# Attention products in a hybrid mLSTM and attention block: float32 against three float16 passes

## The chip, the cores and the metric

One core of a Trainium2 chip runs the whole program. The metric is the time of one execution in device microseconds; the program is one layer of a streaming encoder over 512 tokens of width 2048, with a final norm.

## The reference, cut to what matters

The layer normalises x, modulates it by a conditioning vector, and multiplies by one wide input matrix `w_in`. Its columns feed an mLSTM branch (4 heads of 256), an attention branch (8 heads of 128) and two merge gates. Each branch has an output projection; the merged sum goes through `w_out` and is added to x. Of the attention branch, this is what the change touches:

```python
def chunk_attention_branch(aq, ak, av, az, rel_bias):
    q = to_heads(aq, A_HEADS) * (A_HEAD_DIM ** -0.5)
    ...
        s = jnp.einsum('bhqd,bhkd->bhqk', qj, kb).astype(jnp.float32) + bias
        s = jnp.where(valid, s, -jnp.inf)
        p = jax.nn.softmax(s, axis=-1)
        return jnp.einsum('bhqk,bhkd->bhqd', p.astype(vb.dtype), vb)
    ...
    return from_heads(out) * jax.nn.silu(az)
```

## The kernel before, in words

The large products are already made from two float16 parts of each operand: a value is scaled by a power of two, its high part is rounded to float16, and the low part is what is left. `split` (L142) makes them, ACT the high part at L143 and DVE the low part at L144, which reads the high one. Three passes, high by high, high by low and low by high, are accumulated in one PSUM bank.

A prelude, up to some 165 us, streams `w_ada` and makes the modulation, the normalised h and, in float32, seven first column blocks (`PRE`: q, k and z of heads 0 and 1, and q of head 2). From then on the work runs in units (`plan`, L47). A unit is a block of weights of 1 MB: loaded, squared and summed for its scale (L179, L127, L134 to L139), split, and multiplied with h. `feat_mm` (L394) gives a feature by token result in 48 matmuls of 512 columns, `tok_mm` (L412) a token by feature result in 96 matmuls of 256 columns. The unit "if" (L679) makes the mLSTM's eight gate columns with 192 matmuls of 8 columns. Weights are loaded six units ahead and split four units ahead.

The pipeline (L800 to L822) does for unit i, in program order: its products on PE (`gemm`), the evacuation of unit i − 1 (`evac`), then the side work's steps of the phase "A" (ACT and DVE), the loads, squares and splits for later units, the small matmul for their scales, and last the side work's steps of the phase "P" (PE). So a PE step of the side work stands between two units, and its ACT and DVE step runs beside the next unit's products. The tile framework orders each engine's queue from this program; it may put one unit's splits ahead of side work.

Attention (L442) is such side work. For a head: four score matmuls in float32, for query tiles of 128 rows against the 128, 256, 384 and 512 keys up to them (L463); in the next step the addition of the bias, the maximum, the exponential with its sum, and the scaling (L470 to L476); then ten transposes of probabilities in float32 (L483); then their copies out of PSUM into a part of the array `B` (ACT at L490, DVE at L492, two each, of 512, 384, 256 and 128 columns); then four products with v in float32 (L500); then the product with the gate z (L504). The scores use four of the four banks of one PSUM pool, which transposes and products use after them.

q is evacuated by DVE at L701 with both its scales and the factor of the attention, k by ACT at L704, v by ACT at L714 (two parts for a pair of heads), z at L706 to L709. `times` (L114) makes one-column scale products. At head 6 the attention waits for the gate unit and runs the mLSTM's decays, which are many small float32 matmuls (L526 to L539), before it goes on; the mLSTM's heads follow it. The rest (mLSTM, merge, output projection) isn't touched.

Of the kernel before, what the change touches and what calls it, by code (L numbers as in the profile page):

```python
# [19 lines left out]
P = 128  # L20
# [26 lines left out]
def plan():  # L47
    """The pieces of weights in the order of their use: (kind, index, part)."""
    u = []
    for kind, h in ATT:  # L50
        u += [(kind, h, 0), (kind, h, 1)] if kind == "v" else [(kind, h, 0)]
    for h in range(M_H):
        for kind in ("mq", "mk", "mv", "mo", "mz"):
            u += [(kind, h, 0), (kind, h, 1)]
    for d in range(0, KT, 2):
        u += [("ga", d, 0), ("ga", d + 1, 0), ("pa", d, 0), ("gm", d, 0), ("gm", d + 1, 0), ("pm", d, 0)]
    for b in range(8):
        u += [("out", b, 0), ("out", b, 1)]
    return u


PAIRS = ("v", "mv", "out")
VC = M_DH + 2


@with_exitstack
def block_kernel(ctx: ExitStack, tc: tile.TileContext, A, out):
# [26 lines left out]

    # Two arrays that change their content: one holds the split h, later the split merged branches;
    # the other x and h, then the branches' outputs y, in single tiles of 512 columns.
    hsp = big.tile([P, 2, KT, S], F16, tag="A", name="hsp")
# [16 lines left out]
    def times(a, col, imm, name, n=1):  # L114
        t = small.tile([P, n], F32, tag=f"tm{n}", name=f"tm_{name}", bufs=16)
        if col is None:
            V.tensor_scalar(t, a, imm, None, ALU.mult)
        else:
            V.tensor_scalar(t, a, col, imm, ALU.mult, ALU.mult)
        return t  # L120

# [1 line left out]
    def tot_of(cols, name, tot=None):  # L123
# [6 lines left out]
    def scale_of(tot, name, pool=None):  # L130
        """From a sum of squares: 2^e by which the operand is multiplied, and 2^-e."""
        pool = pool or small
        u = small.tile([P, 1], U32, tag="u", name=f"u_{name}")
        V.tensor_scalar(u, tot[:, 0:1].bitcast(U32), 24, None, ALU.logical_shift_right)  # L134
        kw = {} if pool is const else {"bufs": 12}
        sc = pool.tile([P, 1], F32, name=f"sc_{name}", **({} if pool is const else dict(tag="sc", **kw)))
        V.tensor_scalar(sc.bitcast(I32), u, -8388608.0, 204.0 * 8388608.0, ALU.mult, ALU.add)  # L137
        inv = pool.tile([P, 1], F32, name=f"inv_{name}", **({} if pool is const else dict(tag="inv", **kw)))
        V.tensor_scalar(inv.bitcast(I32), u, 8388608.0, 50.0 * 8388608.0, ALU.mult, ALU.add)  # L139
        return sc, inv  # L140
# [4 lines left out]

# [1 line left out]
    units = plan()  # L147
# [59 lines left out]

# [1 line left out]
    att_pool = tc.tile_pool(name="att", bufs=1)  # L209
# [17 lines left out]
    def ada_load(g, n):  # L227
        """The next n pieces of the columns of w_ada that make shift and scale of a group of tiles."""
        ks = groups[g]
        total = 4 if len(ks) == 2 or ks[0] == KT - 1 else 2  # L230
        cols = 256 * len(ks)
        nj = KT // total
        for _ in range(n):
            m = len(adas[g])
            if m == total:
                return
            t = stage.tile([P, 2048], F32, tag="stage", name=f"ada_{g}_{m}")
            o = m * nj * cols
            if len(ks) == 2:
                nc.sync.dma_start(t[:, 0:nj * cols], A["w_ada2"][ks[0] // 2 - 1][:, o:o + nj * cols])  # L240
            else:
                nc.sync.dma_start(t[:, 0:nj * cols], A["w_ada1"][single.index(ks[0])][:, o:o + nj * cols])
            adas[g].append((t, m * nj, nj, cols))
            if m == total - 1 and ks[0] % 2 == 0:
                wpre_load(ks[0])
# [6 lines left out]
    def matvec(t, a, j0, nj, cols):  # L252
        """a[e] += sum over contraction tiles of silu(c) times a piece of w_ada, in two chains."""
        for n in range(nj):
            j = j0 + n
            d, w = a[j % 2], t[:, n * cols:(n + 1) * cols]
            if j < 2:
                V.tensor_scalar(d, w, sc_c[:, j:j + 1], None, ALU.mult)
            else:
                V.scalar_tensor_tensor(d, w, sc_c[:, j:j + 1], d, ALU.mult, ALU.add)  # L260
            if j == KT - 1:
                V.tensor_tensor(a[0], a[0], a[1], ALU.add)
# [129 lines left out]

# [1 line left out]
    def feat_mm(ps, w, xhi, xlo, nk, o=0, half=None):  # L394
        """ps [feature, token] = w^T x over nk contraction tiles; half() is called half way."""
        for k in range(nk):
# [7 lines left out]
    def tok_step(ps, t, ws, x, k):  # L404
        """One contraction tile of ps [token, 256 columns] for token tile t."""
        w, c = ws[k // 8], slice((k % 8) * 256, (k % 8 + 1) * 256)
# [31 lines left out]

# [1 line left out]
    OFF = [0, 4, 7, 9]  # L440

    def attention():  # L442
# [9 lines left out]
        for h in range(A_H):  # L452
# [7 lines left out]
            for i in range(NT):  # L460
                n = (i + 1) * P
                p = bank(f"s_{h}_{i}")
                PE.matmul(p[:, 0:n], lhsT=q[:, i * P:(i + 1) * P], rhs=k[:, 0:n], start=True, stop=True)  # L463
                ps.append(p)
            yield A_
            s = att.tile([P, 10, P], F32, tag="wt", name=f"s_{h}")
            for i in range(NT):
                n = (i + 1) * P
                si = s[:, ROW[i]:ROW[i] + i + 1, :].rearrange("p a b -> p (a b)")
                V.tensor_tensor(si, ps[i][:, 0:n], bias[h][:, S - n:S], ALU.add)  # L470
                mx = small.tile([P, 1], F32, tag="mx", name=f"mx_{h}_{i}")
# [13 lines left out]
            yield A_  # L485
            pT = B[:, 4:7, :].rearrange("p a (b c) -> p (a b) c", c=P)
            for j in range(NT):
                d = pT[:, OFF[j]:OFF[j] + NT - j, :]
                if j % 2 == 0:
                    ACT.copy(d, pt[j][:, 0:NT - j, :])  # L490
                else:
                    V.tensor_copy(d, pt[j][:, 0:NT - j, :])  # L492
            yield P_
# [5 lines left out]
            for j in range(NT):  # L499
                PE.matmul(po[:, j * P:S], lhsT=v[:, j, vs], rhs=pT[:, OFF[j]:OFF[j] + NT - j, :],  # L500
                          start=(j == 0), stop=(j == NT - 1))
            yield A_
            y = B[:, 8 + h, :]
            V.scalar_tensor_tensor(y, po, fac["z", h], z, ALU.mult, ALU.mult)  # L504
            ACT.activation(junk[:, 0:S], y, AF.Square, accum_out=ssq_y[:, 1, h:h + 1])
            yield P_

# [1 line left out]
    mz = {}  # L509
# [117 lines left out]
    def split_y(b):  # L627
        """Split the outputs of one branch, each tile into the slot that the next one has left."""
        yield P_
# [15 lines left out]
    def gates_of_w_ada():  # L645
        """The output gate's part of the modulation, column block after column block."""
        for g in range(4):
# [13 lines left out]

# [1 line left out]
    PSB = {}  # L663
# [30 lines left out]
    def evac(i):  # L694
        kind, h, part = units[i]
        ps, inv = PSB.pop(i), scs[i][1]
        if kind in "qkz":
            t = qkz_tile(kind, f"{kind}{h}")
            if kind == "q":
                iwh = times(inv, i_h, 1.0, f"u{i}")  # L700
# [10 lines left out]
        elif kind == "v":  # L711
            iwh = times(inv, i_h, 1.0, f"u{i}")
            v = B[:, h % 4:h % 4 + 2, :].rearrange("p a (b c) -> p (a b) c", c=256)
            ACT.activation(B[:, h % 4 + part, :], ps, AF.Copy, scale=iwh)  # L714
            if part == 1:
                sb["v", h // 2] = v
        elif kind == "if":
# [58 lines left out]

# [1 line left out]
    side = []  # L778
# [45 lines left out]

# [1 line left out]
    evac(FIRST_O - 1)  # L826
# [86 lines left out]
def _tiles(w, col, n):  # L913
    """n columns from col on, of [k * 128 + p, :]: [128, k * n]."""
    k = w.shape[0] // P
    return w[:, col:col + n].reshape(k, P, n).transpose(1, 0, 2).reshape(P, -1)


def _unit(i, w_in, kind, h, part):
    """The weights of one unit, [128, 2048]."""  # L920
    half = slice(part * D // 2, (part + 1) * D // 2)
# [75 lines left out]
```

## Time and profile before

| | us |
|---|---|
| median of 3 timed runs | 1629.17 |
| lowest and highest of them | 1628.29 and 1630.04 |
| span of the profiled execution, first to last instruction | 1627.2 |

The profiled execution is one more run of the same program; for it the span alone is given, not a time that could be set beside the runs', and the median of the runs is 2.0 us above the span. In the profile PE is the matmul engine, PEld its weight loads, DVE, ACT and POOL the vector, scalar and general engines. The ends of matmuls are modelled and overlap; the time of a stretch of matmuls is therefore read from start to start. A float32 matmul shows as two PE instructions.

### The profile page before, as it was taken

What the parts mean: (1) busy time and instruction counts of PE and PEld (TensorE: products, weight loads), DVE (VectorE), ACT (ScalarE), POOL (GpSimd) and SP (SyncE); (2) the same over time, 40 slices, a digit from 0 to 9 for tenths busy, and PEclk for the clock granted to TensorE, in tenths of its full rate; (3) what the DMA queues carried; (4) which work ended last, traced back from release to release, by engine and by line L of the source; (5) the groups of instructions that cost most, each with busy time, mean ns of one, the idle gap of its engine ahead of it and who ended that gap; (6) DMA issues with size and microseconds to landing.
All of it is one profiled execution on the core that took longest, in us unless ns stands there. A gap on an engine that the chain in (4) does not pass through costs nothing.

```text
span 1627.2 us, 21216 instructions
## 1 busy us (share of the span) xinstructions
PE 1569.3 (96%) x8862; PEld 895.3 (55%) x8862; DVE 811.2 (50%) x1520; ACT 753.4 (46%) x938; POOL 36.5 (2%) x36
## 2 busy tenths in 40 slices
PE   1799999999999999999999999999999999999997
PEld 0344665755745645646547544444444444468886
DVE  7987644344346445355254337354363533365443
ACT  3225844346345474463472555344353452554432
POOL 4101000000000000000000000000000000000000
PEclk8899999999999999999999999999999999999999
DMA  8896422223222222232222235244252522325103
GB/s 355 303 404 243 163 85 86 85 84 111 78 85 80 102 78 104 79 108 100 73 110 79 78 104 207 104 153 155 103 198 93 205 104 104 127 95 193 53 1 104
DMA packets 37543, 210.47 MB, mean 129 GB/s; under 512 B 5060, under 2 KB 9796, under 8 KB 14408
## 3 DMA queue, kind: packets, MB, share of 16 engines
q1 hardware_dynamic: 37448, 209.12, 35.3%
q8 instruction: 69, 1.13, 0.3%
q14 instruction: 26, 0.21, 0.0%
HBM read 204.91 MB, written 4.19 MB: 129 GB/s over the span
## 4 chain that ended last, share of the span: by engine, by line
PE 94%; DVE 4%; ACT 1%; issue 1%; DMA 0%; SPq 0%; ACTq 0%; DVEq 0%
PE ps L400 20%; PE ps L401 20%; PE ps L402 20%; PE pre L320 5%; PE ps L409 4%; PE ps L408 3%; PE ps L410 3%; PE po L410 3%; PE po L408 3%; PE po L409 3%; PE s L463 1%; PE o L500 1%; PE pn L595 1%; PE kq L579 1%; DVE hsp L144 1%
## 5 line engine op out<-in xcount | busy, mean ns | idle before, releaser
L402 PE MATMUL ps<-hsp,w 128*128 128x512 f16 x1296 | 491.1, 379 | 0.3 <-DVE w L144 0.3
L401 PE MATMUL ps<-hsp,w 128*128 128x512 f16 x1296 | 491.1, 379 | 0.1
L400 PE MATMUL ps<-hsp,w 128*128 128x512 f16 x1296 | 491.0, 379 | 0.0
L144 DVE SCALAR_TENSOR_TENSOR w<-st,sc_w,w 128x2048 f16<-128x2048 f32 x130 | 302.8, 2333 | 161.1 <-ACT w L143 159.1
L143 ACT ACTIVATE w<-st,sc_w 128x2048 f16<-128x2048 f32 x130 | 256.7, 1981 | 94.2 <-DVE sc_w L137 80.9
L179 ACT ACTIVATE junk<-st 128x2048 bf16<-128x2048 f32 x130 | 246.4, 1896 | 20.0 <-DMA st<-in_w_u 17.1
L402 PEld LDWEIGHTS <-w 128*128 128x128 f16 x1552 | 151.7, 98 | 184.0 <-issue 0.6
L400 PEld LDWEIGHTS <-w 128*128 128x128 f16 x1552 | 152.2, 98 | 182.1 <-issue 4.2
L401 PEld LDWEIGHTS <-w 128*128 128x128 f16 x1552 | 151.6, 98 | 175.0 <-issue 2.3
L134 DVE TENSOR_SCALAR u_w<-tot_w 128x1 uint32<-128x1 uint32 x114 | 17.8, 156 | 412.7 <-PE tot_w L127 412.7
L409 PE MATMUL ps<-w,hsp 128*128 128x256 f16 x512 | 140.9, 275 | 0.6 <-DVE w L144 0.6
L410 PE MATMUL ps<-w,hsp 128*128 128x256 f16 x512 | 140.8, 275 | 0.0
L408 PE MATMUL ps<-w,hsp 128*128 128x256 f16 x512 | 140.7, 275 | 0.0
L408 PE MATMUL po<-w,msp 128*128 128x256 f16 x512 | 139.4, 273 | 0.5 <-ACT msp L143 0.5
L409 PE MATMUL po<-w,msp 128*128 128x256 f16 x512 | 139.4, 273 | 0.0
L410 PE MATMUL po<-w,msp 128*128 128x256 f16 x512 | 139.2, 273 | 0.1
L320 PE MATMUL pre<-B,wpre 128*128 128x512 f32 x224 | 101.6, 610 | 12.0 <-ACT B L288 12.0
L402 PE MATMUL ps<-B,w 128*128 128x512 f16 x256 | 97.0, 379 | 0.0
L401 PE MATMUL ps<-B,w 128*128 128x512 f16 x256 | 97.0, 379 | 0.0
L400 PE MATMUL ps<-B,w 128*128 128x512 f16 x256 | 97.0, 379 | 0.0
L762 ACT ACTIVATE thg<-ps,tm_u 128x512 f32<-128x512 f32 x32 | 21.8, 682 | 133.8 <-PE tot_w L127 128.6
L320 PEld LDWEIGHTS pre<-B,wpre 128*128 128x128 f32 x224 | 42.6, 195 | 61.9 <-issue 47.7
(207 smaller groups left out, 1435.2 us busy)
## 6 DMA issues: line engine op xcount, KB each, us to landing
st<-in_w_u SPq DMA_DIRECT2D x129, 1024.0 KB, 4.8
ada<-in_w_ada SPq DMA_DIRECT2D x30, 1024.0 KB, 8.4
gst<-in_w_adag SPq DMA_DIRECT2D x16, 1024.0 KB, 5.0
wpre<-in_w_pre SPq DMA_DIRECT2D x8, 896.0 KB, 9.0
B<-in_xT SPq DMA_DIRECT2D x4, 1024.0 KB, 8.1
xo<-in_x SPq DMA_DIRECT2D x32, 128.0 KB, 3.0
out<-xo SPq DMA_DIRECT2D x16, 256.0 KB, 2.8
ada<-in_w_ada SPq DMA_DIRECT2D x4, 512.0 KB, 4.2
```

Source lines behind the costliest of these rows:

```text
L134: V.tensor_scalar(u, tot[:, 0:1].bitcast(U32), 24, None, ALU.logical_shift_right)
L143: ACT.activation(hi, src, AF.Copy, scale=s_)
L144: V.scalar_tensor_tensor(lo, src, s_, hi, ALU.mult, ALU.subtract)
L179: ACT.activation(junk[:, 0:size[i]], st[i][:, 0:size[i]], AF.Square, accum_out=ssq[i])
L320: PE.matmul(accs[i], lhsT=wpre[k][:, o:o + P], rhs=xT[:, k, :], start=(k == 0), stop=(k == KT - 1))
L400: PE.matmul(ps, lhsT=hi, rhs=xhi(k), start=(k == 0), stop=False)
L401: PE.matmul(ps, lhsT=hi, rhs=xlo(k), start=False, stop=False)
L402: PE.matmul(ps, lhsT=lo, rhs=xhi(k), start=False, stop=(k == nk - 1))
L408: PE.matmul(ps, lhsT=x[:, 0, k, ts], rhs=w[:, 0, c], start=(k == 0), stop=False)
L409: PE.matmul(ps, lhsT=x[:, 0, k, ts], rhs=w[:, 1, c], start=False, stop=False)
L410: PE.matmul(ps, lhsT=x[:, 1, k, ts], rhs=w[:, 0, c], start=False, stop=(k == KT - 1))
L762: ACT.activation(t, ps, AF.Tanh, scale=times(inv, i_h, 0.5, f"u{i}"))
```

## The change

The products of probabilities with v, of all heads, and the scores of heads 3 to 7 are made from float16 parts in three passes. The probabilities are split, times 2 to the 14th, as they leave PSUM after the transposes; v, and q and k of heads 3 to 7, are split as they leave PSUM after their unit, times 2 to the −14th, without the units' scales. Those scales come in later: those of q and k, with the factor of the attention, when the bias is added, that of v in the product with z. The parts lie in the bytes that the float32 values had. Heads 0 to 2 keep float32 scores, because q of them, and k of two, come from the prelude. Comments that went are left out of the diff.

```diff
 VC = M_DH + 2
+H16 = 3
...
-        t = small.tile([P, n], F32, tag=f"tm{n}", name=f"tm_{name}", bufs=16)
+        t = small.tile([P, n], F32, tag=f"tm{n}", name=f"tm_{name}", bufs=48)
...
             for i in range(NT):
-                n = (i + 1) * P
+                n, c = (i + 1) * P, slice(i * P, (i + 1) * P)
                 p = bank(f"s_{h}_{i}")
-                PE.matmul(p[:, 0:n], lhsT=q[:, i * P:(i + 1) * P], rhs=k[:, 0:n], start=True, stop=True)
+                if h < H16:
+                    PE.matmul(p[:, 0:n], lhsT=q[:, c], rhs=k[:, 0:n], start=True, stop=True)
+                else:
+                    PE.matmul(p[:, 0:n], lhsT=q[:, 0, c], rhs=k[:, 0, 0:n], start=True, stop=False)
+                    PE.matmul(p[:, 0:n], lhsT=q[:, 0, c], rhs=k[:, 1, 0:n], start=False, stop=False)
+                    PE.matmul(p[:, 0:n], lhsT=q[:, 1, c], rhs=k[:, 0, 0:n], start=False, stop=True)
                 ps.append(p)
...
-                V.tensor_tensor(si, ps[i][:, 0:n], bias[h][:, S - n:S], ALU.add)
+                if h < H16:
+                    V.tensor_tensor(si, ps[i][:, 0:n], bias[h][:, S - n:S], ALU.add)
+                else:
+                    V.scalar_tensor_tensor(si, ps[i][:, 0:n], fac["s", h], bias[h][:, S - n:S], ALU.mult, ALU.add)
...
-            pT = B[:, 4:7, :].rearrange("p a (b c) -> p (a b) c", c=P)
+            pT = B[:, 4:7, :].rearrange("p a b -> p (a b)").bitcast(F16).rearrange("p (e a c) -> p e a c", e=2, c=P)
             for j in range(NT):
-                d = pT[:, OFF[j]:OFF[j] + NT - j, :]
-                if j % 2 == 0:
-                    ACT.copy(d, pt[j][:, 0:NT - j, :])
-                else:
-                    V.tensor_copy(d, pt[j][:, 0:NT - j, :])
+                b = slice(OFF[j], OFF[j] + NT - j)
+                split(pT[:, 0, b, :], pT[:, 1, b, :], pt[j][:, 0:NT - j, :], 2.0 ** 14)
...
-                PE.matmul(po[:, j * P:S], lhsT=v[:, j, vs], rhs=pT[:, OFF[j]:OFF[j] + NT - j, :],
-                          start=(j == 0), stop=(j == NT - 1))
+                b = slice(OFF[j], OFF[j] + NT - j)
+                for n, (e, f) in enumerate(((0, 0), (0, 1), (1, 0))):
+                    PE.matmul(po[:, j * P:S], lhsT=v[:, e, j, vs], rhs=pT[:, f, b, :],
+                              start=(j == 0 and n == 0), stop=(j == NT - 1 and n == 2))
...
-            V.scalar_tensor_tensor(y, po, fac["z", h], z, ALU.mult, ALU.mult)
+            fz = times(fac["v", h // 2], fac["z", h], 1.0, f"y{h}") if h > 1 else times(fac["v", 0], None, 0.5, f"y{h}")
+            V.scalar_tensor_tensor(y, po, fz, z, ALU.mult, ALU.mult)
...
-            if kind == "q":
+            if kind in "qk" and h >= H16:
+                t = t.bitcast(F16).rearrange("p (e c) -> p e c", e=2)
+                split(t[:, 0, :], t[:, 1, :], ps, 2.0 ** -14)
+                fac[kind, h] = times(inv, i_h, 2.0 ** 14, f"u{i}")
+                if ("q", h) in fac and ("k", h) in fac:
+                    fac["s", h] = times(fac["q", h], fac["k", h], A_DH ** -0.5, f"s{h}")
+            elif kind == "q":
...
-            iwh = times(inv, i_h, 1.0, f"u{i}")
-            v = B[:, h % 4:h % 4 + 2, :].rearrange("p a (b c) -> p (a b) c", c=256)
-            ACT.activation(B[:, h % 4 + part, :], ps, AF.Copy, scale=iwh)
+            v = B[:, h % 4:h % 4 + 2, :].rearrange("p a b -> p (a b)").bitcast(F16)
+            v = v.rearrange("p (e j c) -> p e j c", e=2, c=256)
+            p2 = ps.rearrange("p (j c) -> p j c", c=256)
+            split(v[:, 0, 2 * part:2 * part + 2, :], v[:, 1, 2 * part:2 * part + 2, :], p2, 2.0 ** -14)
             if part == 1:
+                fac["v", h // 2] = times(inv, i_h, 1.0, f"u{i}")
                 sb["v", h // 2] = v
```

## Rows read from the trace of the kernel before

**Rows 1.** The page: busy time, share of the span and instructions of each engine.
```profile
PE 1569.3 (96%) x8862; PEld 895.3 (55%) x8862; DVE 811.2 (50%) x1520; ACT 753.4 (46%) x938; POOL 36.5 (2%) x36
```

**Rows 2.** Busy times by stretch: span, engines busy (instructions), PE clock, DMA share, GB/s.
```profile
165.00:1442.00 1277.00, 1276.06 (x6947) 684.19 (x6945) 579.42 (x1093) 617.99 (x716) 1.89 (x9) 1.00 0.31 110
...
212.00:560.00 348.00, 348.00 (x2183) 212.25 (x2182) 153.59 (x335) 161.86 (x220) 0.21 (x2) 0.99 0.25 87
368.20:371.70 3.50, 3.50 (x36) 2.53 (x34) 1.57 (x6) 2.44 (x6) 0.00 (x0) 0.51 0.77 290
422.80:429.70 6.90, 6.90 (x35) 5.28 (x35) 2.73 (x10) 0.00 (x0) 0.00 (x0) 0.51 0.42 152
```

**Rows 3.** Waits of PE, 165 to 1440 us: total us, times, longest.
```profile
PE ps L409 <- DVE w L144: 0.6, 1, 0.6
PE ps L402 <- DVE w L144: 0.3, 1, 0.3
```

**Rows 4.** Timeline of PE, head 1: start us, us, engine, line, operation, out<-in, shape, count.
```profile
216.40 0.38 PE L400 MATMUL ps<-hsp,w 128*128 128x512 f16 x1
...
226.76 0.17 PE L127 MATMUL tot_w<-ssq,onesb 128*128 128x1 bf16 x1
226.79 2.40 PE L463 MATMUL s<-k,q 128*128 128x128 f32 x8
229.03 0.27 PE L408 MATMUL ps<-w,hsp 128*128 128x256 f16 x1
...
239.51 0.17 PE L127 MATMUL tot_w<-ssq,onesb 128*128 128x1 bf16 x1
...
251.17 2.40 PE L500 MATMUL o<-B 128*128 128x512 f32 x8
253.41 0.38 PE L400 MATMUL ps<-hsp,w 128*128 128x512 f16 x1
```

**Rows 5.** Timeline of PE, gate unit's first matmul and what follows it; groups, weight load.
```profile
363.93 0.17 PE L685 MATMUL ps<-w,hsp 128*128 128x8 f16 x1
...
368.80 2.91 PE L463 MATMUL s<-k,q 128*128 128x128 f32 x6
...
L402 PEld LDWEIGHTS <-w 128*128 128x128 f16 x1552 | 151.7, 98 | 184.0 <-issue 0.6 <-DVE w L144 0.6
```

**Rows 6.** Groups by line and shape: count, busy us, mean ns, idle time before.
```profile
L144 DVE SCALAR_TENSOR_TENSOR B<-B,sc_y 128x512 f16<-128x512 f32 x16 | 12.0, 751 | 9.0 <-ACT B L143 9.0
...
L470 DVE TENSOR_TENSOR s<-s,bias 128x512 f32<-128x512 f32 x8 | 5.4, 680 | 0.4 <-PE s L463 0.4
...
L490 ACT COPY B<-pt 128x512 f32<-128x512 f32 x8 | 4.6, 578 | 7.4 <-PE pt L483 7.4
...
L504 DVE SCALAR_TENSOR_TENSOR B<-o,tm_u,z 128x512 f32<-128x512 f32 x6 | 4.5, 750 | 5.9 <-PE o L500 5.9
L492 DVE COPY B<-pt 128x384 f32<-128x384 f32 x8 | 4.4, 555 | 0.5
...
L701 DVE TENSOR_SCALAR q<-ps,tm_u 128x512 f32<-128x512 f32 x5 | 3.7, 748 | 17.6 <-PE tot_w L127 15.4 <-PE ps L402 2.2
```

**Rows 7.** Timelines of DVE, PE and ACT, head 4: last scaling, transposes, last copy, products.
```profile
345.65 0.49 DVE L476 TENSOR_SCALAR s<-s,sm 128x512 f32<-128x512 f32 x1
...
350.18 1.29 PE L483 MATMUL pt<-ident,s 128*128 128x128 f32 x10
...
353.31 0.37 ACT L490 COPY B<-pt 128x256 f32<-128x256 f32 x1
...
361.69 2.40 PE L500 MATMUL o<-B 128*128 128x512 f32 x8
```

**Rows 8.** Timelines of DVE and PE, head 7: second weight split, last scaling, transposes.
```profile
495.18 2.34 DVE L144 SCALAR_TENSOR_TENSOR w<-st,sc_w,w 128x2048 f16<-128x2048 f32 x1
...
497.44 0.48 DVE L476 TENSOR_SCALAR s<-s,sm 128x512 f32<-128x512 f32 x1
...
497.49 1.47 PE L483 MATMUL pt<-ident,s 128*128 128x128 f32 x10
```

## The prediction

> **What bounds the kernel now.** I read the page's busy times first: TensorE (PE) is busy for 1569.3 of 1627.2 us, while VectorE (DVE) and ScalarE (ACT) are near half [rows 1]. An average over stages can mislead, so the busy times by stretch come next. From 165 us, where the weight-by-weight part begins, to 1442 us, where the last merge ends, PE is busy for 1276.06 of 1277.00 us; in the attention part, 212 to 560 us, for all 348.00 of 348.00, with DVE at 153.59 and ACT at 161.86 [rows 2]. The list of waits, asked for PE alone between 165 and 1440 us, holds two entries, 0.6 and 0.3 us, both on a weight split [rows 3]. So a microsecond of PE work taken out of the attention part should leave the whole span a microsecond shorter: everything behind it is one unbroken stream. The reader is to see that neither a DMA nor ACT or DVE ends a wait of PE there worth counting.
>
> **The products that change.** Per head the scores and the products with v are four matmuls each, of 128 to 512 columns, 1280 columns together. In float32 each is issued as two PE instructions, so the trace shows a block of 8. The timeline gives a block's price as the distance from its first start to the first start of the next work. For scores: 229.03 − 226.79 = 2.24 us; for the products with v: 253.41 − 251.17 = 2.24 us [rows 4].
>
> The new passes are float16 matmuls such as the large products already are. 48 of 512 columns start between 216.40 and 226.76: 0.2158 us each. 96 of 256 columns start between 229.03 and 239.51: 0.1092 us each [rows 4]. The difference is 0.1066 us for 256 columns; along this line 384 columns cost 0.1625 and 128 columns 0.0559 us. No float16 matmul of 128 or 384 columns against full weights stands in the trace, so these two are estimates. Three passes over the four widths cost 3 × (0.2158 + 0.1625 + 0.1092 + 0.0559) = 1.63 us. Each block thus saves 2.24 − 1.63 = 0.61 us. There are 8 blocks with v and 5 of scores (heads 3 to 7): 13 × 0.61 = **7.9 us off PE**. The transposes of the probabilities stay float32 and are not touched.
>
> The doubtful term is the 128-column pass, 39 of them. The trace shows a float16 weight load as a 98 ns record, longer than 56 ns [rows 5]. But in the gate unit each of 192 float16 matmuls of 8 columns has a weight load of its own, and they start between 363.93 and 368.80, 25.4 ns apart [rows 5]. Loads therefore overlap well below 56 ns, and I take 0.0559. The upper bound is 98 ns, where nothing of a load were hidden: 39 × 0.042 = 1.6 us back. The lower bound is the line itself; a matmul below it is excluded, since it would stream columns faster than the 512-column rows do.
>
> The Trainium skill (TensorE: Matmul & The Clock Gate, section "Back-to-back issue gap") speaks against a part of this: in a real stream of load and matmul pairs it gives some 81 ns for 128 columns. By it the gain would be an estimated 39 × 25 ns = 1.0 us smaller. The same sentence gives about 131 ns for 512 columns, where this trace has 216, so I don't follow it.
>
> **What ACT and DVE get in addition.** Every operand must now be split: ACT writes the high part, DVE the low part. Nearest rows: an ACT copy of 512 columns out of PSUM 578 ns, a DVE copy of 384 columns 555 ns, DVE's scaled subtraction of 512 columns 751 ns, its scaled product out of PSUM 750 ns, against 680 ns for the plain addition of the bias [rows 6]. Per head:
> - Probabilities: four ACT and four DVE operations instead of two copies on each. DVE gets about 2.2 instead of 0.84 us, ACT about 1.7 instead of 0.95 (widths by the same straight line).
> - q and k of heads 3 to 7: q, until now 748 ns on DVE, costs that again plus about 0.6 on ACT; k, until now on ACT alone, gets 0.75 on DVE on top [rows 6].
> - v: each of its eight evacuations gets 0.75 us on DVE.
> - The bias addition becomes a scaled one: at most 0.07 us on each of four widths, 0.28 in all.
> - The one-column scale products: some 0.2 us each, two or three a head.
>
> That is about 3.6 us of DVE and 1.4 us of ACT per head, in 37 us from one head to the next. The two have 56 and 53 per cent of that stretch free [rows 2], so as throughput it costs nothing. As latency it counts where PE reads the result. Two places decide:
> - PE's products with v wait for the split probabilities. In head 4 the last copy ends at 353.31 + 0.37 = 353.68 and PE starts the products at 361.69: 8.0 us free [rows 7], and no head has less. The longer chain takes at most 2.2 + 1.7 − 0.5 us more. Cost nothing.
> - PE's transposes wait for the last scaling of the softmax. In head 4 this ends at 345.65 + 0.49 = 346.14, the transposes start at 350.18: 4.0 us free [rows 7]; heads 1 to 6 lie between 4.0 and 5.0, head 0 at 3.4. From head 3 on the transposes come 0.61 us sooner behind the first score (the block in front is shorter) and the additions take 0.28 more: 3.1 us remain. Cost nothing.
> - Head 7 is the exception. There DVE also has the convolution of the next branch and two weight splits. The second, 2.34 us at 495.18, runs ahead of the last scaling, which ends at 497.92, after the transposes have started at 497.49; their block is 1.47 us long [rows 8], against 1.29 in head 4 [rows 7]. Here 0.61 + 0.28 = 0.9 us becomes a new wait of PE, if the order of DVE's queue stays. It could be zero if the scaling is put ahead of that split. I take **0.9**.
>
> If those covers were gone, the extra work would be worth 13 times some tenths of a microsecond and more; this is the slower rival below. No DMA is added or moved, and POOL gets nothing. The larger pool of one-column tiles costs memory, no time. The weight splits come no later than DVE's spare time allows; after head 0 no wait of PE names one [rows 3].
>
> **The sum.** −7.9 + 0.9 = −7.0 us. The profiled execution has a span of 1627.2 us; the median of the runs is 1629.17, that is 2.0 above it, and I keep this surround. 1629.2 − 7.0 = **1622.2 us**.
>
> **The clock.** PE's granted clock falls twice in the attention part: for about 3.4 us from 368.2, behind the gate unit of 8-column matmuls, and for about 6.8 us from 422.8, behind the small matmuls of the decays; each is the lower level, 1.2 GHz (means of 0.51 over stretches a little longer) [rows 2]. Half of such time is lost, 1.7 and 3.4 us. Both causes remain, some 4 to 6 us earlier. If the first fall is missed the gain is 1.7 larger, if one is longer by as much it is that much smaller.
>
> **The rivals.**
> 1. *Weight loads bind the 128-column passes.* For it: 98 ns records; against it: 25.4 ns pitch [rows 5]. 1.6 us back: 1623.8. Chance 0.08. The 81 ns of the Trainium skill (TensorE: Matmul & The Clock Gate, "Back-to-back issue gap") lie between the two; they would give an estimated 1623.2.
> 2. *The clock falls at other places.* The falls come from work that the change moves in time. 1620.5 or 1623.9. Chance 0.14.
> 3. *Slower: the softmax is late for the transposes.* Place: the last scaling of heads 3 to 7, queued on DVE behind weight splits. It decides once more than 3.1 us stand ahead of it that don't now. Head 7 shows the pattern [rows 8]. If two splits (2 × 2.34) and one added low part (0.75) came ahead of it in all five heads, PE would wait 5.43 − 3.1 = 2.3 us each. Without head 7's own 0.9, which is in this, that is 1621.3 + 5 × 2.3 = 1632.8. Against it: about one weight split is made per 10.4 us unit, and DVE stands idle more than half of the time. Chance 0.03.
> 4. *No gain: the time comes back as waits elsewhere.* It needs weights or splits that pace PE. The waits of 0.6 and 0.3 us [rows 3] speak against it, as does DVE's 579.42 of 1277 [rows 2]. It would give about 1629, and so would three-pass products that cost what the float32 ones do. Chance 0.07.
>
> **How the numbers follow.** My forecast has 0.68. The range starts from 1622.2: below, the clock's 1.7, head 7's 0.9 and a little for the median of a few runs give 1619.2; above, 1.6 for the loads and some tenths of new waits, or the clock's 1.7 and the same, give 1625.0. It leaves out the last two rivals and the corners of the others. Some 0.2 per cent, 3.3 us, is what a measurement of this kernel can tell from no change; all cases but the last two are faster by more, 0.90, rival 4 is within it, 0.07, and rival 3 slower, 0.03.
>
> **What would show it.** In the changed profile a block of scores from head 3 on, and every block with v, should hold 12 PE matmuls and last about 1.63 us; scores of heads 0 to 2 stay at 2.24. PE should still be busy for all but one or two microseconds between the prelude and the last merge. DVE's busy time should grow by some 25 us, ACT's by 9, with no effect. The waits of PE should name the softmax's scaling in head 7 and almost nothing else. I am wrong if a block takes 1.8 us or more (loads), if PE waits for the split probabilities or for scalings in several heads (the slower rival), or if the time between head 7 and the end changes, where nothing is edited.

## The result, and the profile after

The changed kernel takes 1618.89 us (median of 4 runs, 1618.45 to 1620.05) against 1629.13 us (4 runs, 1628.29 to 1630.04): a ratio of 0.9939 [0.9925, 0.9952], **10.2 us faster**. The forecast was 1622.2, its range 1619.2 to 1625.0: the sign was right, and the median lies 0.3 us below the range. The profiled execution of the changed kernel took 1620.05 us, the longest of the four, with a span of 1618.0.

First the busy times of the page and the stretches of the changed kernel that answer to [rows 1] and [rows 2]. Columns of the second: stretch, its length, then busy time and count of PE, PEld, DVE, ACT and POOL, PE's mean granted clock, DMA share, GB/s.

```profile
PE 1559.5 (96%) x8914; PEld 889.2 (55%) x8914; DVE 827.7 (51%) x1558; ACT 758.6 (47%) x959; POOL 36.6 (2%) x36
```

```profile
165.00:1433.00 1268.00, 1266.66 (x6998) 678.23 (x6997) 595.86 (x1131) 623.02 (x737) 1.79 (x9) 1.00 0.31 111
212.00:560.00 348.00, 347.60 (x2277) 211.44 (x2275) 172.85 (x378) 172.53 (x250) 0.34 (x4) 0.99 0.25 90
364.40:367.90 3.50, 3.50 (x19) 1.73 (x16) 2.37 (x7) 3.06 (x8) 0.00 (x0) 0.51 0.68 279
419.00:422.60 3.60, 3.60 (x20) 2.59 (x18) 0.98 (x7) 0.00 (x0) 0.00 (x0) 0.53 0.63 262
```

PE is still the bound: busy for 1266.66 of 1268.00 us. DVE has 16.5 us more than before and ACT 5.2, and neither is near the span. The last two rows are where the granted clock is at its lower level (1.2 GHz); their counterparts in [rows 2] are 3.50 us at 0.51 and 6.90 us at 0.51. So the second low stretch is half as long as before.

The list of PE's waits in the changed kernel, 165 to 1433 us (total, times, longest), has one entry more than [rows 3]:

```profile
PE ps L410 <- DVE w L145: 0.6, 1, 0.6
PE pt L492 <- DVE s L485: 0.4, 1, 0.4
PE ps L403 <- DVE w L145: 0.3, 1, 0.3
```

PE's timeline of the changed kernel (start, duration, engine, line, operation, shape, count): the scores of head 3, then its products with v.

```profile
298.61 0.22 PE L467 MATMUL s<-k,q 128*128 128x128 f16 x1
298.66 0.22 PE L468 MATMUL s<-k,q 128*128 128x128 f16 x1
298.71 0.22 PE L469 MATMUL s<-k,q 128*128 128x128 f16 x1
298.77 0.27 PE L467 MATMUL s<-k,q 128*128 128x256 f16 x1
...
299.10 0.33 PE L467 MATMUL s<-k,q 128*128 128x384 f16 x1
...
299.58 0.38 PE L467 MATMUL s<-k,q 128*128 128x512 f16 x1
...
300.23 0.27 PE L409 MATMUL ps<-w,hsp 128*128 128x256 f16 x1
...
322.38 1.79 PE L508 MATMUL o<-B 128*128 128x512 f16 x12
324.00 0.38 PE L401 MATMUL ps<-hsp,w 128*128 128x512 f16 x1
```

Both blocks last 1.62 us from their first start to the next work, against 2.24 in [rows 4]. The 128-column passes start 0.05 to 0.06 us apart (298.61 to 298.77 for three), the 384-column ones 0.16 apart (299.10 to 299.58 for three). All eight blocks with v and the scores of heads 3 to 7 are as long as these, but for head 5's scores, which run at the lower clock and take 3.11 us.

**Where the time went.** All that the change touches lies between the first large product and the first product of the merge gates. What stands behind that is as long in all the profiled executions; what stands ahead of it varies from one execution to the next, whatever the kernel (156.5 to 158.2 us). I call the distance between these two starts the main stretch. These rows end it before and after; it begins at 157.09 before and at 156.99 after.

```profile
1442.61 0.39 PE L836 MATMUL pgate<-dg,ones 128*128 128x128 f32 x2
```

```profile
1433.46 0.39 PE L853 MATMUL pgate<-dg,ones 128*128 128x128 f32 x2
```

It shrinks from 1285.52 to 1276.47 us, by **9.05**. Thirteen blocks by 0.61 are −7.93, head 7's transposes +0.42 (block of 1.30 before, 1.72 after, start to start). What is left, −1.5, goes by this theory to the shorter time at the low clock; the experiments test that.

### The profile page after: what moved, and what is told of

Same layout as the page of the kernel before. It is cut to its first block, busy times and chain, and to the rows that moved or that the text cites. A ratio compares the mean times of both kernels' runs of the same rounds, so it can differ in the third digit from the quotient of the medians.

```text
span 1618.0 us, 21379 instructions
## 1 busy us (share of the span) xinstructions
PE 1559.5 (96%) x8914; PEld 889.2 (55%) x8914; DVE 827.7 (51%) x1558; ACT 758.6 (47%) x959; POOL 36.6 (2%) x36
## 4 chain that ended last, share of the span: by engine, by line
PE 93%; DVE 5%; ACT 1%; issue 1%; DMA 0%; SPq 0%; ACTq 0%; DVEq 0%
PE ps L401 20%; PE ps L402 20%; PE ps L403 20%; PE pre L321 5%; PE ps L410 4%; PE ps L409 3%; PE ps L411 3%; PE po L411 3%; PE po L409 3%; PE po L410 3%; PE pn L604 1%; PE kq L588 1%; PE o L508 1%; DVE hsp L145 1%; DVE ac_z L261 1%
## 5 line engine op out<-in xcount | busy, mean ns | idle before, releaser
L135 DVE TENSOR_SCALAR u_w<-tot_w 128x1 uint32<-128x1 uint32 x114 | 17.8, 156 | 415.4 <-PE tot_w L128 415.4
```

## The experiments

The theory after the result: the blocks pay 0.61 us each whatever else happens; the rest is the clock, whose low time behind the small matmuls of the gate unit and of the decays was 10.2 us before and 6.8 after, half of it lost. The rival: the blocks themselves, or the work around them, are worth more than 0.61. The table has all kernels, with the names that the expectations use; each ratio is to runs of the kernel before in the same round. The low time is worked out from the stretches with a mean clock under 1, as twice the length times what the mean lacks of 1.

| kernel | median, us (lowest to highest, runs) | ratio to before | main stretch, us | at the low clock in the attention part, us |
|---|---|---|---|---|
| before | 1629.13 (1628.29–1630.04, 4) | | 1285.52 | 10.2 |
| before, again (e5) | 1629.03 (1628.08–1629.97, 11) | 1.0001 [0.9992, 1.001] | 1284.87 | 10.2 |
| after | 1618.89 (1618.45–1620.05, 4) | 0.9939 [0.9925, 0.9952] | 1276.47 | 6.8 |
| after, again (e6) | 1619.21 (1618.51–1620.45, 5) | 0.994 [0.9928, 0.9953] | 1275.94 | 6.8 |
| products with v only (e1) | 1623.58 (1623.01–1624.17, 5) | 0.9966 [0.9954, 0.9979] | 1279.17 | 6.8 |
| scores only (e2) | 1625.05 (1624.23–1627.34, 8) | 0.9977 [0.9967, 0.9987] | 1281.11 | 6.8 |
| before, filled (e3) | 1647.66 (1646.68–1648.68, 4) | 1.0116 [1.01, 1.0131] | 1303.28 | none |
| after, filled (e4) | 1639.09 (1638.81–1639.74, 5) | 1.0061 [1.0049, 1.0074] | 1295.70 | none |
| small matmuls spread (e7) | 1616.85 (1616.69–1617.40, 5) | 0.9925 [0.9912, 0.9939] | 1273.48 | none |
| spread, and two more edits (e8) | 1616.18 (1616.05–1617.77, 5) | 0.9923 [0.9911, 0.9936] | 1273.09 | none |
| the same, scaling on ACT (e9) | 1614.66 (1614.45–1616.04, 5) | 0.9915 [0.9901, 0.9928] | 1271.22 | none |

### One half of the change at a time

The products with v alone (all scores stay float32):

```diff
-H16 = 3
+H16 = 8
```

> Only the products with v are split, the scores of all heads stay float32. Theory (each float16 block saves 0.61 us, the rest of the measured gain comes from shorter falls of PE's clock): 8 x 0.61 = 4.9 us below the kernel before, 1624.2, and up to 1.7 us more where a fall is shorter; 8 blocks of 1.63 us in the trace, head 7's transposes as before (1.30 us). Rival (a block saves more than its length shows, or the gain is made outside the attention part): 8/13 of 10.2 = 6.3 us, with falls as long as before.

Measured: 1623.58 us. The main stretch is 6.35 us shorter than before: 8 × 0.61 = 4.88, and 1.47 more. The transposes of head 7 last 1.31 us and wait for nothing that the list of waits shows, as was to be expected with the softmax as it was.

The scores alone (the copies of the probabilities, v and the products as before the change):

```diff
-                split(pT[:, 0, b, :], pT[:, 1, b, :], pt[j][:, 0:NT - j, :], 2.0 ** 14)
+                if j % 2 == 0:
+                    ACT.copy(d, pt[j][:, 0:NT - j, :])
+                else:
+                    V.tensor_copy(d, pt[j][:, 0:NT - j, :])
...
-                for n, (e, f) in enumerate(((0, 0), (0, 1), (1, 0))):
...
+                PE.matmul(po[:, j * P:S], lhsT=v[:, j, vs], rhs=pT[:, OFF[j]:OFF[j] + NT - j, :],
+                          start=(j == 0), stop=(j == NT - 1))
```

> Only the scores of heads 3 to 7 are split, the products with v stay float32. Theory: 5 x 0.61 = 3.05 us, less 0.4 of a longer wait in head 7's transposes, so 2.6 us below the kernel before, 1626.5, and up to 1.7 us more where a fall of the clock is shorter. Rival (gain proportional to the blocks): 5/13 of 10.2 = 3.9 us, with falls as long as before.

Measured: 1625.05 us. The main stretch is 4.41 us shorter: 5 × 0.61 = 3.05 less 0.42 for head 7, whose block is 1.72 here, are 2.63; 1.78 more are there again. The stretches of both half changes (the columns as above), products with v first, then scores:

```profile
366.50:370.10 3.60, 3.60 (x27) 2.60 (x24) 1.90 (x7) 2.81 (x7) 0.00 (x0) 0.53 0.80 291
421.00:424.70 3.70, 3.70 (x21) 2.72 (x21) 2.07 (x9) 0.00 (x0) 0.00 (x0) 0.54 0.81 283
```

```profile
366.20:369.80 3.60, 3.60 (x49) 2.35 (x46) 2.21 (x6) 2.35 (x5) 0.00 (x0) 0.53 0.82 296
420.90:424.60 3.70, 3.70 (x21) 2.69 (x21) 2.10 (x9) 0.00 (x0) 0.00 (x0) 0.54 0.82 283
```

In each, in the one profile that there is, both low stretches are 3.4 us long, so the second is shorter than before, and 1.5 to 1.8 us go with it. The two halves add up to 10.76 us of main stretch where the whole has 9.05: the difference of 1.7 is about what one low stretch costs, a gain that each half shows and the whole has once. The sizes alone don't part theory from rival, which gave 6.3 and 3.9 us where the main stretches show 6.35 and 4.41; but the rival had falls as long as before, and they are shorter. Executions of one kernel differ here too: of the scores alone, two of the eight runs took 1627.1 and 1627.3 us, about 3 us more than the traced one with its 1624.23.

### No fall of the clock in either kernel

If the rest is the clock's, two kernels whose clock doesn't fall must differ by the blocks and head 7 alone. In both, matmuls of 512 columns into an unread PSUM bank are set between the small ones, 48 in the gate unit and 52 in the decays. They are added work. The same edit goes into the kernel before and into the changed one:

```diff
                     PE.matmul(ps, lhsT=h_lo[:, k, ts], rhs=hi, start=False, stop=(k == KT - 1))
+                    if (t * KT + k) % 4 != 3:
+                        PE.matmul(dmy, lhsT=h_hi[:, k, ts], rhs=h_hi[:, k, :], start=True, stop=True)
...
+        def more(n=2):
+            for e in range(n):
+                PE.matmul(dmy, lhsT=h_hi[:, e, 0:P], rhs=h_hi[:, e, :], start=True, stop=True)
...
                 PE.matmul(pr[0:4, t * P:(t + 1) * P], lhsT=src[:, t, :], rhs=rhs, start=True, stop=True)
+                more()
```

> The kernel before, with 48 products of 512 columns that nobody reads put between the gate unit's small matmuls and 52 between those of the decays, so that PE's clock should not fall there. They cost 100 x 0.216 = 21.6 us. If both falls go (1.7 and 3.4 us in the profiled execution), the kernel is 16.5 us slower than before, 1645.6; if the falls cost nothing, 21.6 us, 1650.7. If the clock still falls, the trace shows it and the run says nothing on them.

> The changed kernel with the same 100 products put in. Theory: without falls the change is worth its blocks alone, 13 x 0.61 - 0.4 = 7.5 us below e3, 1638.1. Rival (falls don't matter to the gain): 10.2 us below e3.

The stretch from 355 to 460 us of both, before first:

```profile
355.00:460.00 105.00, 105.00 (x779) 61.70 (x778) 33.77 (x71) 42.57 (x50) 0.10 (x1) 1.00 0.21 73
```

```profile
355.00:460.00 105.00, 105.00 (x803) 61.50 (x801) 36.86 (x77) 43.15 (x54) 0.10 (x1) 1.00 0.21 74
```

The clock is 1.00 throughout in both. Their main stretches end here, at the first product of the merge gates (they begin at 156.58 and 156.56):

```profile
1459.86 0.61 PE L849 MATMUL pgate<-dg,ones 128*128 128x128 f32 x4
```

```profile
1452.26 0.61 PE L866 MATMUL pgate<-dg,ones 128*128 128x128 f32 x4
```

The difference is 1303.28 − 1295.70 = **7.58 us**, where 7.93 − 0.42 = 7.51 was worked out. With the clock out of play, the change is worth what its blocks and its one wait say. (The medians, 2.1 and 1.0 us above what was expected, differ by 8.6; the four runs of the filled kernel before spread over 2 us, and the traced one is the fastest of them.) Both filled kernels came out about 1 us longer in the main stretch than 100 × 0.216 less the recovered clock (17.8 and 19.2 measured, 16.5 and 18.2 worked out). Eleven pairs of the added matmuls, those between float32 matmuls of 128 columns, take 0.54 us from start to start where the other pairs take 0.43; that is 1.2 us, the same in both, and drops out of the difference.

### Both kernels again

No edit; a second profile of each shows how far the low stretches belong to the kernel and how far to the execution.

> The kernel before once more, for its clock. Theory (the gain beyond the blocks is shorter falls): two or three low stretches of 3.4 us in the attention part, as in its first profile, and each one more in an execution costs 1 to 1.7 us. Rival: the same number of low stretches as in the changed kernel, so they explain nothing.

> The changed kernel once more. Theory: one or two low stretches of 3.4 us in the attention part, median within 0.5 us of 1618.9, head 7's transposes 1.72 us again. Rival: two or three, as before the change, with the same median.

The low stretches of the kernel before, and then of the changed one, in these executions:

```profile
366.00:373.00 7.00, 7.00 (x103) 4.81 (x100) 2.68 (x8) 4.14 (x9) 0.00 (x0) 0.51 0.43 152
...
424.10:427.70 3.60, 3.60 (x20) 2.61 (x18) 1.84 (x9) 0.00 (x0) 0.00 (x0) 0.53 0.79 284
```

```profile
362.90:369.80 6.90, 6.90 (x70) 3.78 (x67) 3.11 (x10) 4.94 (x10) 0.00 (x0) 0.51 0.49 167
369.80:430.00 60.20, 60.20 (x415) 40.13 (x414) 26.21 (x60) 30.86 (x38) 0.10 (x1) 1.00 0.25 91
```

The kernel before has its long stretch at the gate unit this time and its short one at the decays; the changed kernel has one long stretch at the gate unit and none at the decays. The places vary, the sums don't: 10.2 us before, 6.8 after, in two profiles of each, as the theories had it. Head 7's transposes take 1.71 us again. The main stretches differ by 8.93 us in this pair, by 9.05 in the first.

Equal low time doesn't cost the same everywhere: the second profiles' main stretches are 0.65 us (before) and 0.53 us (after) shorter than the first ones'. In the kernel before, again, the 192 matmuls of the gate unit take 4.96 us up to the next work (363.35 to 368.31), although 2.2 us of that are at the low clock; in the changed kernel's first profile, where none of it is, they take 4.83 (359.55 to 364.38). So hardly anything is lost while these 8-column matmuls run.

### The small matmuls spread among large ones

If small matmuls in a row are what brings the clock down, the same matmuls set between large ones should not. No work is added. Three quarters of the gate unit's matmuls go between those of the unit before it, those of the decays between the 256-column matmuls of v of heads 6 and 7:

```diff
-    def feat_mm(ps, w, xhi, xlo, nk, o=0, half=None):
+    def feat_mm(ps, w, xhi, xlo, nk, o=0, half=None, each=None):
...
+            if each:
+                each(k)
...
+                each = lambda k: gate_mm(UIF, 3 * k, 3 * k + 3)
...
+            gate_mm(i, 48, 64)
```

> The changed kernel with the same work in another order on PE: three quarters of the gate unit's small matmuls stand between the large ones of the unit before, and the decays' small matmuls between large ones of the first part of v of heads 6 and 7. Theory: PE's clock no longer falls there; against the changed kernel 1.7 us for each low stretch it had (one or two), less up to 0.7 us because head 5's scores now follow head 4's products more closely: 1615.5 to 1617.5. Rival (falls cost nothing): 1618.9 or more.

The stretch from 340 to 460 us, which holds both places:

```profile
340.00:460.00 120.00, 120.00 (x888) 70.38 (x887) 58.86 (x127) 55.63 (x77) 0.10 (x1) 1.00 0.29 103
```

The clock is 1.00. The main stretch is 2.99 us shorter than in the changed kernel, 2.46 shorter than in its second profile. Against the first, start by start, each of the two places gives 1.67 us, together about half of 6.8; 0.35 us goes back where the decays' matmuls stand among v's: that unit takes 16.78 us with them (400.22 to 417.00), against 16.43 when they stood behind it (401.58 to 418.01). The median falls from 1618.89 to 1616.85, inside the forecast.

### Two more edits, and a wait that came back

The scores of heads 1 and 2 get the three passes too (the float32 q of both and k of head 1 are split again in SBUF, k of head 2 leaves PSUM in two parts; q and k get a buffer more), and the last scaling of head 7, for which PE waits, goes to POOL:

```diff
-                V.tensor_scalar(si, si, sm, None, ALU.mult)
+                (nc.gpsimd if h == A_H - 1 and i == NT - 1 else V).tensor_scalar(si, si, sm, None, ALU.mult)
...
+                    split(t[:, 0, :], t[:, 1, :], sb[kind, h + 1], 2.0 ** 4)
```

> e7, with head 7's last scaling of the softmax on POOL instead of DVE, and with float16 scores for heads 1 and 2 too, whose q and k from the prelude are split again later, from SBUF. Theory: 0.6 us from head 7's transposes (1.72 to 1.12) and 2 x 0.61 us from the scores, so 1.8 us below e7. Rival (what ACT and DVE get more is not covered by PE's stream): no faster than e7.

Measured: 1616.18 us, 0.7 below the spread kernel. In the main stretch it is 0.39: the scores of heads 1 and 2 last 1.63 us each and give their 1.22, head 7 takes 1.25 back, and 0.4 comes from a shorter wait on a weight split before 195 us (0.3 instead of 0.6 in the list of waits). The timelines of POOL, DVE and PE in this kernel, in which [idle <-X] is the wait and its releaser:

```profile
482.70 3.54 POOL L500 TENSOR_SCALAR s<-s,sm 128x512 f32<-128x512 f32 x1 [93.40 <-DVE u L766]
```

```profile
482.46 2.34 DVE L145 SCALAR_TENSOR_TENSOR w<-st,sc_w,w 128x2048 f16<-128x2048 f32 x1
```

```profile
484.14 0.49 PE L507 MATMUL pt<-ident,s 128*128 128x128 f32 x3
486.29 0.98 PE L507 MATMUL pt<-ident,s 128*128 128x128 f32 x7 [1.66 <-POOL mv L780]
487.11 0.38 PE L411 MATMUL ps<-hsp,w 128*128 128x512 f16 x1
```

The scaling takes POOL 3.54 us, where DVE takes 0.48 in [rows 8]; PE starts again at 486.29, just behind its end at 486.24. (The profile names a small memset that POOL ran right behind it.) For its first 2.1 us a weight split of DVE ran beside it; how much of the 3.54 is due to that isn't shown. Head 7's transposes grew from 1.72 to 2.97 us (484.14 to 487.11).

The same with that scaling on ACT:

```diff
-                (nc.gpsimd if h == A_H - 1 and i == NT - 1 else V).tensor_scalar(si, si, sm, None, ALU.mult)
+                if h == A_H - 1 and i == NT - 1:
+                    ACT.activation(si, si, AF.Copy, scale=sm)
```

> e8 with head 7's last scaling on ACT instead of POOL, whose 3.54 us made the transposes wait 1.7 us. Theory: head 7's transposes back to about 1.12 us, so 1.8 us below e8 in the trace's main stretch, 1614.4 as the median. Rival (the scaling waits for its reciprocal behind the weight split on whatever engine it runs): the transposes still wait, 1616.

ACT's row of the scaling and PE's of the transposes, in this kernel:

```profile
481.84 0.72 ACT L501 ACTIVATE s<-s,sm 128x512 f32<-128x512 f32 x1 [1.85 <-DVE u L769]
```

```profile
483.41 1.25 PE L510 MATMUL pt<-ident,s 128*128 128x128 f32 x10
484.50 0.38 PE L411 MATMUL ps<-hsp,w 128*128 128x512 f16 x1
```

The scaling ends before the transposes start, and their block is 1.09 us long; the rival, in which they still wait, didn't come. The main stretch is 1.87 us shorter than with POOL, where 1.8 was forecast. This kernel, **1614.66 us**, is the fastest here: 4.2 us below the changed one, 14.5 below the kernel before.

## Why the prediction was right, and where it failed

**The blocks: right.** 0.61 us each was forecast; with the clock's falls out of the way the two filled kernels differ by 7.58 against 7.51. PE's stream stayed unbroken, so each block's microseconds reached the end.

**The 128-column passes: right.** 0.0559 us was taken and 0.05 to 0.06 is seen, so the first rival, weight loads, is refuted: they don't show in a stream in which each matmul has a load of its own (PE and PEld have 8914 instructions each). By the 81 ns that the Trainium skill (TensorE: Matmul & The Clock Gate, "Back-to-back issue gap") gives for such a stream, three of these starts would have taken an estimated 0.24 us; they took 0.16. The trace doesn't agree with that figure; its other one there, the isolated formula (columns at 2.4 GHz and some 2.5 ns), does fit, with 55.8 ns.

**ACT and DVE: right that they are covered, too high in size.** DVE got 16.5 us, not 25, and ACT 5.2, not 9. Part of this is how busy time counts: the durations of DVE's instructions add up to 20.4 us more than before and ACT's to 8.2, but neighbours overlap in the trace, and busy time has the overlap once. The rest, on DVE, is prices: the one-column products grew by 1.7 us, where the prediction's prices make some 4, and the low parts that read PSUM are cheaper than the 751 ns that stood for them in [rows 6], as these groups of the changed kernel show (line, operation, shape, count, then busy time and mean ns).

```profile
L145 DVE SCALAR_TENSOR_TENSOR k<-ps,k 128x512 f16<-128x512 f32 x5 | 3.4, 687 | 0.0
...
L145 DVE SCALAR_TENSOR_TENSOR B<-pt,B 128x512 f16<-128x512 f32 x8 | 5.5, 682 | 0.0
```

No wait of PE names a split of the probabilities, of v, q or k. The slower rival, a softmax that is late in five heads, didn't come, and neither did the one without a gain.

**Head 7: the right place, half the size.** Only there does PE wait for the last scaling. The term was +0.9; it measured +0.42. DVE's timeline of the changed kernel, PE's, and the work that follows the transposes of [rows 8] before:

```profile
486.85 2.35 DVE L145 SCALAR_TENSOR_TENSOR w<-st,sc_w,w 128x2048 f16<-128x2048 f32 x1
489.12 0.48 DVE L485 TENSOR_SCALAR s<-s,sm 128x512 f32<-128x512 f32 x1
```

```profile
488.54 0.71 PE L492 MATMUL pt<-ident,s 128*128 128x128 f32 x5
489.66 0.77 PE L492 MATMUL pt<-ident,s 128*128 128x128 f32 x5 [0.41 <-DVE s L485]
490.26 0.38 PE L401 MATMUL ps<-hsp,w 128*128 128x512 f16 x1
```

```profile
498.79 0.38 PE L400 MATMUL ps<-hsp,w 128*128 128x512 f16 x1
```

The order in DVE's queue is the one foreseen, a weight split ahead of the scaling. But the delay was smaller: the scaling ends 1.06 us behind the first transpose (489.60 and 488.54), against 0.43 before (497.92 and 497.49), so 0.63 us later and not 0.9. And not all of it is a wait: six of the ten transposes don't need the last query tile's row, and five run ahead of the wait here, where three did before (whose block, 1.30 us against 1.12 in head 4, held some 0.2 of wait already); at 0.11 us each the two more take 0.2 off.

**The clock: the step that failed.** The prediction said "Both causes remain, some 4 to 6 us earlier" and put the low time into the sum as unchanged. The causes did remain, and came 4.4 us earlier at the gate unit. But the low time fell from 10.2 to 6.8 us in both profiles of each kernel, and 1.5 us more than blocks and head 7 explain came off the main stretch (1.5 to 1.8 in the halves). The end of the decays, where the second fall comes, with the product behind it and the next small one, before and after:

```profile
422.57 1.62 PE L539 MATMUL p_cols<-lf,tri 128*128 128x4 f32 x8
424.05 0.37 PE L408 MATMUL ps<-w,hsp 128*128 128x256 f16 x1
...
437.35 0.34 PE L552 MATMUL p_m<-ident,mrow 4*128 4x4 f32 x3
```

```profile
417.12 1.03 PE L548 MATMUL p_cols<-lf,tri 128*128 128x4 f32 x8
418.01 0.27 PE L409 MATMUL ps<-w,hsp 128*128 128x256 f16 x1
...
430.25 0.34 PE L561 MATMUL p_m<-ident,mrow 4*128 4x4 f32 x3
```

Between the first and the last of these starts nothing is edited, and yet there are 14.78 us before and 13.13 after: −1.65. From the gate unit to head 5's transposes it is 19.00 and 18.53 (363.93 to 382.93, 359.55 to 378.08), that is 0.61 for head 5's block and +0.14. Together this is the −1.5.

The second rival, falls at other places, had this price at its lower end, 1620.5; its two ends together had a chance of 0.14. With 1.7 for the clock and head 7's true size the sum is 1622.2 − 1.7 − 0.5 = 1620.0. The median is 1.1 us below that.

Why the low time is shorter is **not settled**. The small matmuls are the same and in the same order. Before, the second fall comes while the last of them still run (the last eight instructions take 1.48 us, start to start); after, it comes 1 us behind them (they take 0.89), as the stretch from 419.0 shows. The length goes with that in all eleven falls of the six profiles that have any: the three that began 1.2 to 2.2 us before the small matmuls ended lasted 6.8 us, the eight that began later, from 0.6 us before their end on, lasted 3.4. But the moment differs between executions of one kernel: at the gate unit of the kernel before, the fall comes 0.6 us before the end in one profile and 2.2 in the other. What sets it, and whether the change makes the earlier fall rarer or these few executions happened so, no run shows.

**About a microsecond is left.** The medians differ by 10.2, and by 9.8 in the repetition; the main stretches by 9.05 and 8.93. The stretch ahead of it, which differs by 0.1 us in each pair, doesn't explain it. In part it lies in which executions were traced: the first profile of the changed kernel is the longest of its four runs (1620.05), the second of the kernel before the shortest of its eleven (1628.08), and both make the traces differ by less than the medians. The changed kernel's faster runs may have one low stretch fewer, but no trace here shows one, and the runs' mean granted clocks don't settle it: its four fastest runs (1618.45 to 1618.87 us) have 0.989 where its two slowest have 0.988, yet in the kernel before runs of 1628.6 to 1629.0 us have 0.986 and slower ones 0.987.

## What to carry to other kernels

Where one engine's stream has no gaps, price an edit from that engine's starts in the trace and add up: this was good to 0.1 us here where the clock didn't fall, with latency needing a look only where the operand is late. Count stretches at the lower clock as work of their own, and look at what shifts when earlier work shrinks; two profiles of the same kernel show how much of it is the execution's. Rows of tiny matmuls were better spread among large ones than run by themselves (2.0 us here), and a short operation that PE waits for is moved to an engine that is both free and quick at it.

## What the runs showed of the hardware that was not expected

TensorE's clock falls to its lower level with PE busy all the time: 3.50 of 3.50 us at 0.51 [rows 2], as 192 matmuls of 8 columns come to their end [rows 5]. The Trainium skill (TensorE: Matmul & The Clock Gate, "HAM oscillation — how this bites in real kernels") ties such falls to waits of the engine between bursts; here no wait precedes them, and what removes them is wider matmuls in between, added (the filled kernels) or moved there (the spread one). At the low clock, matmuls of 8 columns lose almost nothing: 4.96 against 4.83 us for 192, with 2.2 us of it at half the clock. And POOL took 7 times as long as DVE for the scaling of 512 columns, 3.54 against 0.48 us; since a DVE split ran beside it, and three scalings of this shape in the prelude took POOL 1.93 us on average, 3.54 is not POOL's price by itself.
